# Keys and values of heads 4 to 7 as pairs in seven products, and old-cache logits by wide products and sums, in a float32 hybrid decoder step

## The chip, the cores and the metric

The kernel runs on one core of one Trainium2 chip. The core has a matrix engine (TensorE, PE), a vector engine (VectorE, DVE), a scalar engine (ScalarE, ACT), GpSimd (POOL), and SyncE (SP), which here only issues DMA. The metric is the device time of one execution in microseconds (us); the time of a kernel is the median of several executions. One execution is also recorded by the hardware profiler. Times in the profile count from the start of the recorded span.

## The reference

One inference step of a decoder layer with two parallel branches, on 512 prompt tokens with 16 learned meta tokens ahead of them, and on 8 sample sequences of 4 new tokens each, which have 512 old positions in a paged cache. Everything is float32; the model width is 2048, with 8 heads of 128.

```python
h = rmsnorm(x, g_pre)
q, k, v, ga, cb, cc, ch, gc, ma, mc = jnp.split(h @ w_in, split_offsets(), axis=-1)
a = attend(q, k, v, b_sb).reshape(bsz, t, D_ATTN) * jax.nn.silu(ga)
c = cb * causal_conv(u_ext, w_conv, b_conv) * jax.nn.silu(gc)        # u = cc * ch with its history
merged = (jax.nn.sigmoid(ma + b_gate[:D_MODEL]) * (a @ w_pa)
          + jax.nn.sigmoid(mc + b_gate[D_MODEL:]) * (c @ w_pc))
y = x + rmsnorm(merged @ w_out, g_post)
```

The attention breaks a stick: with z = q k / sqrt(128) + b, the weight of position s for query t is sigmoid(z_ts) times the product of (1 - sigmoid(z_tj)) over the positions j between s and t, worked out in log space. For the samples the keys and values are those of the cache's pages and the new ones. Keys and values of all tokens and the last two inputs of the convolution are outputs too.

## The kernel before, in words

**Matrix products.** A float32 product is made from three products of a faster matrix format. `w_split` (line 237) cuts a block of weights into a high part (`whi`, cast on ScalarE, line 240) and a remainder (`wlo`, a subtraction on VectorE, line 241); the normalised tokens stand in memory in the same two parts, `h_hi` and `h_lo`, 16 blocks of 128 rows by 560 token columns. Each block of the inner dimension takes three matmuls: high by high, high by low, low by high. Three buffers hold split weights (`whl`), five hold loaded ones (`wraw`).

`proj` (line 271) projects onto 128 columns: 16 blocks, two halves of 280 tokens, three matmuls each, so 96 (line 256). `pair` (line 1012) projects onto 256 columns. It cuts weights and tokens into 2 x 2 blocks and forms the result in `seven` (line 974) from seven products of half the inner dimension in place of eight: seven times 8 x 3 = 24 matmuls (line 971), with sums of weight blocks (lines 983, 986, 994, 999) and of results (997, 1002) on VectorE. The block sums of the tokens, `t_hi` and `t_lo`, are made once ahead of the pairs (lines 936 to 956), and the difference of two token blocks then takes the place of one block inside `h_hi` and `h_lo`: direct projections have to be done by then.

**Order of the program.** Norm and queries of heads 0 to 3; then `head_now` for heads 0 to 3: keys, values, the queries of a later head, and attention over the prompt. Then `head_later` for heads 4 to 7: only keys and values, by direct projections, with copies put in DRAM (`k_scr`, `vn_scr`) for their attention later on. Then the token block sums; then 36 pairs: 4 of the attention gate, 16 of the convolution (4 groups of 4), 16 of the two output gates. Behind them come the attention of heads 4 to 7 among the products with `w_pc`, the products with `w_pa`, and the last product with `w_out`, also by sevens.

**The samples' attention over the cache** runs beside this as a generator, `decode_steps` (line 759). It goes through 16 units (two halves of four heads, eight sequences). A unit loads its queries, repeated over all partitions (`qb`), and four pages of keys (`kpage`, three buffers), and forms the logits on VectorE, one instruction per page, query and head: multiply 128 keys-by-channel elements by the query and sum them up (line 781; the sum is written by a second record, the read of the accumulator). That is 16 instructions per page. The generator stops after each page. The calls `dec_step` and `dec_group` (lines 891 to 906) place its steps in the program: the first `DEC1` = 6 units among heads 0 to 7, the other ten among the first 25 pairs; behind them come the weights (after pairs 26 to 28) and the products with the values.

**What sets the order.** A planner orders the instructions of each engine by its own costs; the order of the program counts among those that are ready in its plan. `pin` (`keep_in_program_order`) ties an instruction behind the one written before it on the same engine, so that it can't be moved ahead of that one. At run time each engine and each DMA queue works strictly in the planned order. Loads of weights go through SP's queue; page loads and all stores of this stage go through POOL's queue, so a page load that waits for a buffer holds up what stands behind it.

Of the kernel before, what the change touches and what calls it, by code (L numbers as in the profile page):

```python
# [17 lines left out]
P = 128  # L18
# [24 lines left out]
H = 8  # L43
# [4 lines left out]
DEC1 = 6  # L48
# [12 lines left out]
def hybrid_step_kernel(  # L61
# [499 lines left out]
    def k_proj(h):  # L561
        o = proj(GATE_K + h * P, ALL)
        kr = hp.tile([P, T], F32, name="raw", bufs=2)
        for ob, s in nparts(o):
            act.copy(kr[:, s], ob)
# [6 lines left out]
        pe.matmul(zz, lhsT=kr[:, TP:T], rhs=qs_all[:, h, :], start=True, stop=True)  # L572
# [4 lines left out]
    def v_proj(h, pl=None):  # L577
        o = proj(GATE_V + h * P, ALL)
        vr = hp.tile([P, T], F32, name="raw", bufs=2)
        for ob, s in nparts(o):  # L580
            act.copy(vr[:, s], ob)
# [5 lines left out]
        if pl is None:  # L587
            pool.dma_start(vn_scr[h][0:512].rearrange("(a p) d -> p a d", p=P), vn[:, 0:4, :])
            pool.dma_start(vn_scr[h][512:TP], vn[0:16, 4, :])
            return None  # L590
        return v_split(pl, vn)
# [126 lines left out]
    def head_now(h):  # L718
# [40 lines left out]
    def decode_steps():  # L759
# [3 lines left out]
        for said, part in (("part", units[:DEC1]), ("logits", units[DEC1:])):  # L763
            with tc.tile_pool(name="dec1", bufs=2, side="right") as d1:
                for hf, b in part:
# [8 lines left out]
                    for pg in range(NPG):  # L774
                        kt = d1.tile([P, 512], F32, name="kpage", bufs=3)
                        first(page_load(kt, kc, b, pg, cs))
                        for i, qt in enumerate(qts):
                            for t in range(2):
                                for h in range(4):
                                    junk = d1.tile([P, P], F32, name="junk", bufs=2)  # L780
                                    dve.tensor_tensor_reduce(  # L781
                                        out=junk, in0=kt[:, h * P:(h + 1) * P], in1=qt[:, t, h * P:(h + 1) * P],
                                        scale=1.0, scalar=0.0, op0=ALU.mult, op1=ALU.add,
                                        accum_out=z_all[:, pg, b, 4 * hf + h, 2 * i + t:2 * i + t + 1])
# [713 lines left out]
```

## Time and profile before

| | |
|---|---|
| time before, median of 3 runs (lowest, highest) | 1581.93 us (1581.13, 1584.88) |
| the profiled execution, its own time | 1584.74 us |
| span of its trace | 1583.1 us |
| TensorE busy | 1560.7 us |
| VectorE busy | 1268.5 us |
| ScalarE busy | 761.7 us |
| first and last logit instruction of line 781 | 122.0 us, 945.5 us |

How to read the rows below. In the groups a row names line, engine, operation, output <- inputs, shapes and count; behind the bar stand the busy time in us and the mean of one in ns, then the idle time of the engine just before them and what ended it. In sums by stage there is a stretch of time and for each engine its busy time with the number of instructions; then the granted clock of TensorE as a share (`PEclk`), the busy share of the DMA engines, and the rate. The rows in order of time have the start, the duration, engine, line and operation. A waits row says which engine and line waited for which, for how long in total, how often, and the longest. Matmul ends are modelled, so a matmul's busy time says less than the step from one start to the next.

### The profile page before, as it was taken

The page shows a single profiled execution, that of the slowest core. Times are in us where ns is not written, and L with a number is a line of the kernel's source. Part 1 is how long each engine was busy: PE and PEld are TensorE (multiplying, and loading weights), DVE is VectorE, ACT ScalarE, POOL GpSimd, SP SyncE. Part 2 cuts the span into 40 slices and gives each one's busy share as a digit, 9 for nine tenths or more (in the row PEclk, how much of TensorE's full clock was granted, in tenths as well). Part 3 has the DMA queues.
Part 4 walks back from the last instruction along what each step waited for, and adds up shares of the span by engine and source line. Part 5 has one row for each costly group of instructions (what it writes and reads, how often), then busy time and mean ns, then how long its engine had stood idle before and what let it go on. Part 6 is the DMA issues. An engine that isn't in the chain of part 4 may idle for free.

```text
span 1583.1 us, 32334 instructions
## 1 busy us (share of the span) xinstructions
PE 1560.7 (99%) x12172; PEld 1527.5 (96%) x12172; DVE 1268.5 (80%) x3574; ACT 761.7 (48%) x1345; POOL 234.7 (15%) x428
## 2 busy tenths in 40 slices
PE   8999999999999999999999999999999999999997
PEld 7999999999999999999999999898899999999997
DVE  7329999956799999999999997565678857877776
ACT  6245555435444444444444457444476734345552
POOL 1123333222111010011011102312100010000000
PEclk9999999999999999999999999999999999999999
DMA  8245556344454544445465545767595455433345
GB/s 263 82 137 186 168 160 184 107 130 136 150 180 124 151 130 140 146 134 162 120 181 173 162 138 168 245 194 226 157 306 172 148 178 165 152 107 94 101 143 183
DMA packets 300674, 252.77 MB, mean 160 GB/s; under 512 B 11521, under 2 KB 268613, under 8 KB 299701
## 3 DMA queue, kind: packets, MB, share of 16 engines
q1 hardware_dynamic: 272021, 160.45, 35.1%
q0 software_dynamic: 28368, 89.98, 17.0%
q8 instruction: 95, 1.56, 0.4%
q14 instruction: 62, 0.51, 0.1%
q10 hardware_dynamic: 128, 0.27, 0.1%
HBM read 217.95 MB, written 32.71 MB: 158 GB/s over the span
## 4 chain that ended last, share of the span: by engine, by line
PE 94%; DVE 2%; ACT 1%; DMA 1%; issue 1%; DVEq 0%; SPq 0%; ACTq 0%
PE mm L971 32%; PE mm L256 27%; PE o L971 24%; PE mm L321 2%; PE z L702 1%; PE o L714 1%; PE z L321 1%; PE tp L856 1%; DMA raw<-in_w_in 1%; PE z L620 1%; PE z L1439 1%; PE tp L505 0%; PE z L1293 0%; DVE wlo L241 0%; DMA at<-a_scr 0%
## 5 line engine op out<-in xcount | busy, mean ns | idle before, releaser
L240 ACT CAST whi<-raw 128x1024 fp32r<-128x1024 f32 x247 | 259.4, 1051 | 375.5 <-PE mm L971 135.0
L241 DVE TENSOR_TENSOR wlo<-raw,whi 128x1024 fp32r<-128x1024 f32 x247 | 301.7, 1222 | 90.2 <-ACT whi L240 88.0
L971 PE MATMUL mm<-h_hi,whi 128*128 128x272 f32 (+1 forms) x1152 | 333.5, 289 | 0.7 <-ACT whi L240 0.7
L971 PE MATMUL mm<-h_hi,wlo 128*128 128x272 f32 (+1 forms) x1152 | 332.6, 290 | 0.0
L971 PE MATMUL mm<-h_lo,whi 128*128 128x272 f32 (+1 forms) x1152 | 332.5, 289 | 0.0
L971 PE MATMUL o<-t_hi,whi 128*128 128x272 f32 (+1 forms) x864 | 251.6, 291 | 3.3 <-DVE c L997 3.3
L971 PE MATMUL o<-t_lo,whi 128*128 128x272 f32 (+1 forms) x864 | 251.2, 291 | 0.0
L971 PE MATMUL o<-t_hi,wlo 128*128 128x272 f32 (+1 forms) x864 | 251.1, 291 | 0.0
L781 DVE CUSTOM_DVE_ANT_0 junk<-kpage,qb 128x128 f32<-128x128 f32 x1024 | 246.0, 287 | 4.0 <-DMA qb<-q_scr 3.7
L971 PEld LDWEIGHTS mm<-h_hi,whi 128*128 128x128 f32 x1152 | 217.4, 189 | 6.1 <-ACT whi L240 3.5
L971 PEld LDWEIGHTS mm<-h_lo,whi 128*128 128x128 f32 x1152 | 216.8, 188 | 0.9 <-issue 0.8
L971 PEld LDWEIGHTS mm<-h_hi,wlo 128*128 128x128 f32 x1152 | 217.0, 189 | 0.2
L240 ACT CAST whi<-s 128x1024 fp32r<-128x1024 f32 x126 | 132.0, 1048 | 151.2 <-PE mm L971 48.5
L241 DVE TENSOR_TENSOR wlo<-s,whi 128x1024 fp32r<-128x1024 f32 x126 | 154.2, 1224 | 62.8 <-ACT whi L240 61.3
L256 PE MATMUL mm<-h_lo,whi 128*128 128x280 f32 (+1 forms) x640 | 187.6, 293 | 0.0
L256 PE MATMUL mm<-h_hi,wlo 128*128 128x280 f32 (+1 forms) x640 | 187.1, 293 | 0.0
L256 PE MATMUL mm<-h_hi,whi 128*128 128x280 f32 (+1 forms) x640 | 186.7, 292 | 0.0
L971 PEld LDWEIGHTS o<-t_hi,whi 128*128 128x128 f32 x864 | 164.1, 190 | 4.0 <-DVE c L997 4.0
L971 PEld LDWEIGHTS o<-t_hi,wlo 128*128 128x128 f32 x864 | 164.5, 190 | 0.9 <-issue 0.8
L971 PEld LDWEIGHTS o<-t_lo,whi 128*128 128x128 f32 x864 | 164.8, 191 | 0.0
L256 PEld LDWEIGHTS mm<-h_lo,whi 128*128 128x128 f32 x640 | 120.3, 188 | 0.8
L256 PEld LDWEIGHTS mm<-h_hi,wlo 128*128 128x128 f32 x640 | 120.5, 188 | 0.5
(452 smaller groups left out, 3166.7 us busy)
## 6 DMA issues: line engine op xcount, KB each, us to landing
raw<-in_w_in SPq DMA_DIRECT2D x192, 512.0 KB, 4.5
kpage<-in_cache_k POOLq DMA_DIRECT2D x64, 256.0 KB, 3.8
qb<-q_scr POOLq DMA_DIRECT2D x32, 512.0 KB, 5.7
vpage<-in_cache_v POOLq DMA_DIRECT2D x64, 256.0 KB, 5.7
raw<-in_w_out SPq DMA_DIRECT2D x32, 512.0 KB, 4.0
gate_scr<-g POOLq DMA_DIRECT2D x32, 272.0 KB, 4.9
gt<-gate_scr POOLq DMA_DIRECT2D x16, 544.0 KB, 4.5
raw<-in_w_pc SPq DMA_DIRECT2D x16, 512.0 KB, 4.7
```

The source lines that it names most:

```text
L240: act.copy(hi, x)
L241: dve.tensor_sub(lo, x, hi.bitcast(F32))
L256: pe.matmul(o, lhsT=w, rhs=r[:, t0:t1], start=(k == 0 and n == 0), stop=(k == nk - 1 and n == 2))
L321: pin(pe.matmul(o, lhsT=l, rhs=r[:, k, t0:t1], start=(start and m == 0), stop=(stop and m == 2), skip_group_check=True))
L620: pe.matmul(zt[:m, c0:c0 + n], lhsT=l[:, s0:s0 + m], rhs=r[:, ts:ts + n], start=(c0 == 0 and i == 0), stop=(i == 2), skip_group_check=True)
L702: pe.matmul(o, lhsT=l, rhs=x, start=False, stop=(i == len(ops) - 1), skip_group_check=True)
L714: pe.matmul(ot[:, ts - NMETA:ts - NMETA + n], lhsT=l[:m, st, :], rhs=x[:m, c0:c0 + n], start=False, stop=(g == GROUPS[-1] and i == 2), ski ...
L781: dve.tensor_tensor_reduce(out=junk, in0=kt[:, h * P:(h + 1) * P], in1=qt[:, t, h * P:(h + 1) * P], scale=1.0, scalar=0.0, op0=ALU.mult, o ...
L856: pin(pe.matmul(po[32 * j:32 * (j + 1), :], lhsT=lhs, rhs=rhs, start=(pg == 0), stop=last and n >= len(vts) - 4, tile_position=(0, 32 * j) ...
L971: pe.matmul(o, lhsT=l[:, k, :], rhs=r, start=(start and k == 0 and m == 0), stop=(stop and k == 7 and m == 2), skip_group_check=True)
L1439: pin(pe.matmul(o, lhsT=(m1, m2)[h][:, k + 8 * (q == 1), ts], rhs=two[h][q == 2][:, :, k, :], start=(n == 0), stop=(n == 47)))
```

## The change

Three things change together.

1. `head_later` is replaced by `heads_later`: keys of heads 4 and 5, values of heads 4 and 5, then the same for heads 6 and 7, each as a `pair` in seven products. These four pairs stand behind the token block sums, which are 280 columns wide per half now (274 before), and ahead of the gates. The projections of the queries of heads 4 to 7 leave `head_now` and stand directly behind it.
2. A page's logits: for each half of its four queries one product of 128 x 1024 elements with the page repeated (`kq`), then a sum along the channels on VectorE; of the second half's two queries the second is summed on ScalarE by four accumulating copies. Products and sums on VectorE are pinned.
3. The generator stops four times a page. `DEC1` is 2: two units among heads 0 to 3, fourteen among the pairs, one step after each of the seven products and at the end of a pair (`dec_tick`), from the second pair to the 29th of now 40. The weights come after pairs 30 to 32.

Also, the mask for the later heads (`after`) is made later, and the token sums are formed in another order.

```diff
-DEC1 = 6
+DEC1 = 2
...
@@ head_now
         khi, klo = k_split(np_, k_proj(h))
-        dec_step(1 if h else 0, "part")
+        qhi, qlo = q_split(np_, qr)
+        dec_step(4 if h else 1, "part")
         vhi, vlo = v_proj(h, np_)
-        dec_step(1, "part")
-        q_proj(NOW + h)
-        dec_step(2, "part")
-        ot = next(attend(np_, h, khi, klo, vhi, vlo, *q_split(np_, qr)))
-        dec_step(2, "part")
+        dec_step(4, "part")
+        ot = next(attend(np_, h, khi, klo, vhi, vlo, qhi, qlo))
...
-    def head_later(h):
-        pool.dma_start(k_scr[h], k_proj(h))
-        dec_step(2, "part")
-        v_proj(h)
-        dec_step(2, "part")
+    def heads_later(h, qs):
+
+        for c, out in ((GATE_K, "k"), (GATE_V, "v")):
+            raws = [hp2.tile([P, T], F32, name="raw", bufs=2) for _ in range(2)]
+            seen = []
+            for m, half, b in pair(c + h * P, HC):
+                act.copy(raws[m][:, NMETA + half * HQ:NMETA + (half + 1) * HQ], b[:, HM:])
+                act.copy(raws[m][:, half * HM:(half + 1) * HM], b[:, :HM])
+                seen.append(m)
+                if seen.count(m) < 2:
+                    continue
+                if out == "k":
+                    pool.dma_start(k_scr[h + m], raws[m])
+                    k_out(hp2, h + m, raws[m], qs[:, h + m - NOW, :])
+                else:
+                    vn = v_out(hp2, h + m, raws[m])
+                    pool.dma_start(vn_scr[h + m][0:512].rearrange("(a p) d -> p a d", p=P), vn[:, 0:4, :])
+                    pool.dma_start(vn_scr[h + m][512:TP], vn[0:16, 4, :])
+            dec_group()
...
@@ decode_steps, per page
+                        if pg == 0 and (hf, b) == part[0]:
+                            yield
                         for i, qt in enumerate(qts):
-                            for t in range(2):
-                                for h in range(4):
-                                    junk = d1.tile([P, P], F32, name="junk", bufs=2)
-                                    dve.tensor_tensor_reduce(
-                                        out=junk, in0=kt[:, h * P:(h + 1) * P], in1=qt[:, t, h * P:(h + 1) * P],
-                                        scale=1.0, scalar=0.0, op0=ALU.mult, op1=ALU.add,
-                                        accum_out=z_all[:, pg, b, 4 * hf + h, 2 * i + t:2 * i + t + 1])
-                        yield
+                            kq = d1.tile([P, 2, 4, P], F32, name="kq", bufs=2)
+                            pin(dve.tensor_mul(kq, qt.rearrange("p t (h d) -> p t h d", d=P),
+                                               kt.rearrange("p (h d) -> p h d", d=P).unsqueeze(1)
+                                               .broadcast_to([P, 2, 4, P])))
+                            yield
+                            nt = 2 - i
+                            zt = z_all[:, pg, b, 4 * hf:4 * hf + 4, 2 * i:2 * i + nt]
+                            if i:
+                                for h in range(4):
+                                    act.activation(kq[:, 1, h], kq[:, 1, h], AF.Copy,
+                                                   accum_out=z_all[:, pg, b, 4 * hf + h, 3:4])
+                            pin(dve.reduce_sum(zt.rearrange("p h t -> p t h"), kq[:, 0:nt], axis=mybir.AxisListType.X))
+                            yield
...
@@ dec_group
-        if n <= 25:
-            dec_step((0, 2, 2, 2)[n - 1] if n <= 4 else 1 if n <= 20 else 4, "logits")
-        else:
-            dec_step(2 if n in (26, 28) else 1)
+        if n == 1:
+            dec_step(1, "logits")
+        elif n == 29:
+            dec_step(64, "logits")
+        elif n > 29:
+            dec_step(2 if n in (30, 32) else 1)
+
+    def dec_tick():
+
+        if 1 <= n_group[0] < 29:
+            dec_step(1, "logits")
...
     for h in range(NOW, H):
-        head_later(h)
+        q_proj(h)
     dec_step(64, "part")
...
@@ seven
         product(x, w_split(w11), rb(0, 0), True, False)
+        tick()
         dve.tensor_add(s, w21, w22)
         product(q, w_split(s), rb(0, 1), True, False)
+        tick()
...
@@ ahead of the gates
+    with tc.tile_pool(name="heads2", bufs=1) as hp2:
+        qs = hp2.tile([P, H - NOW, TS], F32, name="qs")
+        for h in range(NOW, H):
+            pool.dma_start(qs[:, h - NOW, :], qt_scr[h][:, PQ:TQ])
+        for h in range(NOW, H, 2):
+            heads_later(h, qs)
```

More of the change, by code (lines that the diff above doesn't have):

```diff
@@ L559, in v_split, with raw_of, k_out @@
         return vhi, vlo
[L561 to L563 removed]
+    def raw_of(o):
+        raw = hp.tile([P, T], F32, name="raw", bufs=2)
         for ob, s in nparts(o):
[L565 removed]
+            act.copy(raw[:, s], ob)
+        return raw
+    def k_out(hp, h, kr, qs):
         kn = hp.tile([P, 5, P], F32, name="nat", bufs=2)
@@ L571, in k_proj, with v_out @@
         zz = z_ps()[0:TS, 0:TS]
-        pe.matmul(zz, lhsT=kr[:, TP:T], rhs=qs_all[:, h, :], start=True, stop=True)
+        pe.matmul(zz, lhsT=kr[:, TP:T], rhs=qs, start=True, stop=True)
         act.activation(z_new[:, :, h, :], zz.rearrange("p (b t) -> p b t", t=DT), AF.Identity,
                        bias=bsb[0:TS, h:h + 1])
-        return kr
[L577 to L581, printed above, removed]
+    def k_proj(h):
+        kr = raw_of(proj(GATE_K + h * P, ALL))
+        k_out(hp, h, kr, qs_all[:, h, :])
+        return kr
+    def v_out(hp, h, vr):
         vn = hp.tile([P, 5, P], F32, name="nat", bufs=2)
@@ L948, in hybrid_step_kernel @@
             t_split(part(t_hi[0]), part(t_lo[0]), x)
+        for c in range(0, 8, 2):
+            x, y = part(x1), tsp.tile([P, 2, HC], F32, name="y")
             dve.tensor_sub(y, part(h_f, 0, 0), x)
```

41 lines of the change are left out of this document (23 added, 18 removed).

## The prediction

> **What bounds the kernel now.** I read the page first (shares of the engines and the chain that ended last), then sums by stage, then the order in time on VectorE (DVE) and TensorE (PE) inside the stage that the change fills.
>
> ```profile
> PE 1560.7 (99%) x12172; PEld 1527.5 (96%) x12172; DVE 1268.5 (80%) x3574; ACT 761.7 (48%) x1345; POOL 234.7 (15%) x428
> DVE  7329999956799999999999997565678857877776
> PE 94%; DVE 2%; ACT 1%; DMA 1%; issue 1%; DVEq 0%; SPq 0%; ACTq 0%
> ```
>
> TensorE sets the end: 94% of the chain. The 80% of VectorE is an average; slices 4 to 8 and 12 to 23 stand at 9. The stages, cut where the work changes (us from the start; busy time of each engine):
>
> ```profile
> core 0: us, PE busy (x) PEld busy (x) DVE busy (x) ACT busy (x) POOL busy (x), PEclk, DMA share, GB/s
> 75.00:365.00 290.00, 290.00 (x2231) 283.09 (x2230) 227.89 (x1014) 138.23 (x280) 88.47 (x164) 1.00 0.50 151
> 440.00:946.00 506.00, 505.18 (x4000) 504.76 (x4000) 485.65 (x1634) 227.82 (x336) 52.44 (x91) 1.00 0.50 148
> 946.00:1170.00 224.00, 222.24 (x1734) 204.50 (x1734) 143.51 (x171) 116.43 (x166) 48.63 (x87) 0.99 0.68 209
> ```
>
> From 440 to 946 us lie pairs in seven products (gates and convolution) with most of the old-cache logits between them. There VectorE works 485.65 of 506 us: TensorE is still the bound, with 20 us to spare. After 946, when the logits are done, VectorE has 80 us idle in 224. The pace of TensorE, from the chain in order of time (start, length, what):
>
> ```profile
> 211.11 8.99 PE mm L256 x70
> ...
> 454.73 5.83 PE mm L971 x46
> ...
> 944.86 5.79 PE mm L971 x46
> ```
>
> A matmul of 280 columns costs 8.99/70 = 0.1284 us. Between the two lower rows lie 23 pairs: (944.86 - 454.73)/23 = 21.31 us for a pair of 7 x 24 = 168 matmuls. The stage holds 4000/168 = 23.8 pairs.
>
> How VectorE spends its time there (start, duration, what; instructions overlap, so the step from start to start is the price, not the duration):
>
> ```profile
> 444.97 1.23 DVE L983 TENSOR_TENSOR s<-raw 128x1024 f32<-128x1024 f32 x1
> 446.11 0.29 DVE L781 CUSTOM_DVE_ANT_0 junk<-kpage,qb 128x128 f32<-128x128 f32 x1
> 446.32 0.09 DVE L781 DVE_READ_ACCUMULATOR2_ANT z_all<- 128x1 f32 x1
> 446.32 0.29 DVE L781 CUSTOM_DVE_ANT_0 junk<-kpage,qb 128x128 f32<-128x128 f32 x1
> 446.53 0.08 DVE L781 DVE_READ_ACCUMULATOR2_ANT z_all<- 128x1 f32 x1
> 446.53 1.22 DVE L241 TENSOR_TENSOR wlo<-raw,whi 128x1024 fp32r<-128x1024 f32 x1
> 447.67 1.22 DVE L994 TENSOR_TENSOR raw<-raw 128x1024 f32<-128x1024 f32 x1
> 448.80 0.29 DVE L781 CUSTOM_DVE_ANT_0 junk<-kpage,qb 128x128 f32<-128x128 f32 x1
> ```
>
> A two-tensor operation on 1024 elements steps on after 1.14, 1.14 and 1.13 us, 0.09 us before its shown end. A logit instruction steps on after 0.21 us, the read of its accumulator included, although 0.29 and 0.09 are shown for the two. One page for four heads is 16 of them: 3.36 us, not the 6 us to which the durations add up.
>
> **The change, part by part.**
>
> *Matmuls removed.* Keys and values of heads 4 to 7 are eight projections of 2 x 16 x 3 = 96 matmuls of 280 columns; as four pairs they are 4 x 168 = 672 in place of 768. 96 x 0.1284 = 12.3 us less on the bounding engine. Their transposes, outputs and products with the sample queries stay.
>
> *VectorE inside the K and V pairs.* A pair has seven remainders of casts, four block sums of 1024 and two subtractions, where two direct projections had four remainders.
>
> ```profile
> L997 DVE TENSOR_TENSOR c<-o,s 128x272 f32<-128x272 f32 x28 | 12.3, 439 | 4.4 <-PE o L971 4.4
> L511 DVE COPY ks<-tp 32x128 f32<-32x128 f32 x16 | 4.3, 270 | 0.0
> ```
>
> A subtraction steps on after 0.44 - 0.09 = 0.35 us, a small copy of the natural layout after 0.2. That is 11 x 1.14 + 0.7 = 13.2 us against 4.6; with two logit pages (below, 8.1) and four small copies, 22.1 us. TensorE needs 168 x 0.1284 = 21.6 us and the transposes on top:
>
> ```profile
> 356.12 0.60 PE L505 MATMUL tp<-ident,raw 128*128 128x128 f32 x4
> 356.65 0.25 PE L572 MATMUL z<-qs_all,raw 128*32 128x32 f32 x2
> 356.83 0.40 PE L256 MATMUL mm<-h_lo,whi 128*128 128x280 f32 x1
> ```
>
> 356.12 to 356.83 is 0.71 us, with the two small transposes about 1 us per head: 23.6 us for a pair. VectorE fits under it with 1.5 us, so I charge nothing; without that cover, 4 pairs x 2 us.
>
> *A logit page.* Removed: 16 instructions, 3.36 us. Added: two products of 1024 elements, a sum over 1024, a sum over 512, and four accumulating copies on ScalarE. A product with a repeated operand stands nowhere in the trace; its nearest row is the plain product, 1.14, which I take. Nor is there a sum of this width; the nearest:
>
> ```profile
> L1315 DVE TENSOR_REDUCE ss<-og_a x3: 167/171/203, 1563.1 to 1573.0; 128x1 f32<-128x16 f32 x2, 128x3 f32<-128x48 f32 x1
> L1286 ACT ACTIVATE sq<-z x62: 257/278/384, 1407.8 to 1572.5; 128x128 f32<-128x128 f32 x60, 128x256 f32<-128x256 f32 x2
> L1286 ACT ACTIVATION_READ_ACCUMULATOR sq<-z x62: 184/194/201, 1408.0 to 1572.8; 128x1 f32 x62
> ```
>
> ```profile
> L473 DVE TENSOR_SCALAR lo<-e 128x416 f32<-128x416 f32 x12 | 4.5, 372 | 0.8 <-ACT r L470 0.8
> L474 DVE TENSOR_TENSOR lo<-e,lo 128x416 f32<-128x416 f32 x12 | 7.1, 591 | 0.1
> ```
>
> The small reductions take about 169 ns for 16 elements and 203 for 48: 1.06 ns for each further element. So 1024 elements take 169 + 1008 x 1.06 = 1.24 us and step on after 1.15, 512 after 0.61. A page is then 2 x 1.14 + 1.15 + 0.61 = 4.04 us. Bounds: at the rate of a one-input operation (591 - 372 = 219 ns saved on 416 elements, 0.53 ns each, 0.8 us on 1536) it is 3.2 us; above, if a sum costs a tenth more than its slope says, 4.2 us. I take 4.04, since the row is of the operation itself. So the wide form costs VectorE 0.7 us more per page, even with a quarter of the sums on ScalarE.
>
> The Trainium skill (VectorE: DVE Perf Modes, "Rules for kernel authors") speaks for such a rewrite: chained operations should not be fused for speed, their number should be kept small, since each pays its own drain. The steps of 0.21 us above are shorter than the shown durations, so the trace doesn't bear it out for these. What it would give is a rival below.
>
> *Where the pages lie.* Before, 24 pages belong to heads 0 to 3 and 40 to the pairs; now 8 and 56. The ticks run in 28 pairs, the last three of K and V and 25 behind them, eight to a pair; four make a page: two pages a pair. Taking 16 pages out of heads 0 to 3 frees VectorE there, but TensorE is busy 290.00 of 290.00 us, so nothing is won. The queries of heads 4 to 7 move from inside these heads to behind them. They cover the token block sums, 13 x 4 operations of 0.65 us:
>
> ```profile
> L934 DVE TENSOR_TENSOR t_lo<-x,t_hi 128x548 fp32r<-128x548 f32 x8 | 5.7, 719 | 1.4 <-ACT t_hi L933 1.4
> ```
>
> 34 us under four projections of 96 x 0.1284 = 12.3 us; I charge nothing. Heads 0 to 3 lose a quarter of what fills their waits on exponentials: nothing, or up to 3 us a head.
>
> *The 25 gate and convolution pairs with ticks.* Work other than logits on VectorE in the stage: 485.65 - 605 x 0.21 = 358.6 us, over 23.8 pairs 15.07 us each (the logits' 605 instructions with as many accumulator reads are the 1210 of this row, overlaps included):
>
> ```profile
> 440.00:946.00 506.00, 148.28 (x1210) 1.00 0.50 148
> ```
>
> With two pages: 15.07 + 8.08 = 23.15 us a pair against 21.31 on TensorE. 25 x 1.84 = 46 us too much. The products and sums are tied behind the last VectorE instruction written before them and are ready (three page buffers), so I expect them to run in their place; the next remainder then comes later, and TensorE waits for it.
>
> ```profile
> POOL kpage L757 <- DVE z_all L781: 277.9, 33, 16.1
> ACT whi L240 <- PE mm L971: 84.1, 70, 1.8
> DVE wlo L241 <- ACT whi L240: 13.2, 37, 1.0
> ```
>
> To this come VectorE's own waits for a cast, 13.2 us in this stage (last row): 14 us for 25 pairs, between none and twice that. ScalarE's waits for a free weight slot (second row) vanish. Three slots let two products of 3 us run ahead once: -6.
>
> *Queues.* Page loads already make POOL's queue wait up to 16.1 us (first row). A page now lives four ticks, 10.7 us; the outputs of a K or V pair stand behind these loads, and the single buffer of the sample rows makes VectorE's copy of the second head wait for them. Hidden as long as the planner spaces them; if not, up to 3 us for each of 4 pairs. ScalarE gets four copies and four accumulator reads a page, at most 4 x 0.47 = 1.9 us, 3.8 of a pair's 21.3, beside 227.82 of 506 us: room enough, though a cast may stand behind them. The other edits (wider token blocks, a separate query tile, the later mask) come to under 1 us in idle time.
>
> *Sum:* -12.3 + 46 + 14 - 6 = +42 us. The profiled execution took 1584.74 us (span 1583.1), so 1626.7; it lies 2.8 us above the median of the runs shown, 1581.93, on which I put the prediction: 1624 us.
>
> **The rivals.**
>
> *ScalarE's accumulations delay the casts as well.* Two quartets a pair, each up to 1.9 us ahead of a cast; were half of that lost in 25 pairs: 25 x 2 x 0.9 = 45 us in place of the 14 counted, so 1624 + 31 = 1655 us. For it: the cast of a block sum can't be issued early, and its engine works in order. Against: other remainders can fill the gap.
>
> *The logits fall back rather than hold up the weights.* The tie keeps an instruction from being early, not from being late. If the planner lets them slip, the 60 us too much go into the 80 us that VectorE has idle after 946, and only the removed matmuls show: 1581.9 - 12.3 = 1570 us. It decides as long as the products with the values behind the logits still end before the gates do. Against: the loads are ahead, so the steps are ready in their place.
>
> *Small instructions pay in full.* If each logit instruction cost its shown 0.29 + 0.09 us, a page would fall from 6.1 to 2 x 1.22 + 1.24 + 0.70 = 4.4 us, the stage's other work would be 485.65 - 605 x 0.38 = 256 us, 10.7 a pair, and 10.7 + 8.8 = 19.5 us would fit under 21.31: 1570 us. Sums at the one-input rate come out the same within 4 us (15.07 + 6.4 = 21.5). Against: the steps, and the slope of the reductions. This is the case of the Trainium skill's rule named above.
>
> *About even.* Two thirds of the overload hidden by deeper running ahead, the waits filled: 15 - 12.3 = +3, 1585 us.
>
> **How the numbers follow.** Overload as summed 0.58 (its own range 1593 to 1646: 3.7 to 4.2 us a page, waits of 0 to 28 us); casts late as well 0.15; logits fall back 0.13; cheap pages 0.07; about even 0.07. Under 0.3% (4.7 us) a measurement of this kernel can't tell from no change. Faster 0.20, within 0.05, slower 0.75 (0.58, 0.15 and the upper part of the even case). The range goes from the cheap end, 1570, to the second case, 1655.
>
> **What would show it.** Right: in the convolution pairs TensorE's waits end at the remainder of L241 on VectorE; a pair takes 23 us or more there; VectorE has next to no idle time while the logits last; the wide products step on after 1.14 us, the sums after 1.15 and 0.61; the 280-wide direct matmuls are 768 fewer, those of pairs 672 more. Wrong: pairs keep 21.3 us; the logits end well after the 29th pair; a sum of 1024 steps on in under 0.8 us; or TensorE waits in heads 0 to 3, which have fewer projections to fill them.

## Result and profile after

The changed kernel takes 1673.57 us, the median of four runs (1669.96 to 1676.09), against 1581.53 us before: a ratio of 1.0576, with a 95% interval of 1.0551 to 1.0602. It is slower, by 92 us, where 42 us had been forecast (1624 us). The profiled execution took 1669.96 us with a span of 1668.4; the span before was 1583.1, so the two traces differ by 85.3 us, and this is the difference that the readings below divide up.

The page of the changed kernel, its busy times, the slices of VectorE and of the granted clock, and the chain that ended last:

```profile
PE 1573.3 (94%) x12076; PEld 1526.1 (91%) x12076; DVE 1334.2 (80%) x1818; ACT 849.8 (51%) x1879; POOL 237.9 (14%) x432
...
DVE  7257667799899999999999997665668876887776
...
PEclk9999997899999999999999999999999999999999
...
PE 49%; DVE 18%; issue 7%; ACT 4%; DMA 4%; POOL 1%; DVEq 0%; SPq 0%; POOLq 0%; ACTq 0%
```

There are 96 matmuls fewer, as counted (12172 to 12076). TensorE is busy 94% of the span and no longer 99%, and its share of the chain falls from 94% to 49%. VectorE stands at 9 in all but one of the slices 9 to 24, and in slices 7 and 8 the granted clock dips to 7 and 8 tenths. The stages show two places (us from the start; busy time of PE, PEld, DVE, ACT, POOL with counts; granted clock):

```profile
core 0: us, PE busy (x) PEld busy (x) DVE busy (x) ACT busy (x) POOL busy (x), PEclk, DMA share, GB/s
75.00:265.00 190.00, 189.37 (x1440) 183.23 (x1439) 116.59 (x192) 106.65 (x263) 54.06 (x105) 1.00 0.40 120
265.00:303.00 38.00, 0.00 (x0) 0.00 (x0) 37.28 (x56) 12.69 (x25) 2.53 (x5) 0.56 0.01 2
...
485.00:830.00 345.00, 322.02 (x2419) 313.21 (x2418) 333.31 (x393) 164.66 (x429) 36.77 (x63) 0.98 0.46 138
830.00:1005.00 175.00, 166.07 (x1265) 162.31 (x1264) 165.86 (x186) 93.31 (x222) 18.31 (x32) 0.98 0.50 149
1005.00:1246.00 241.00, 240.66 (x1898) 223.25 (x1898) 154.47 (x173) 122.11 (x171) 49.89 (x89) 1.00 0.63 194
```

**The hole.** From 265 to 303 us TensorE runs not one matmul, while VectorE is busy 37.28 of 38 us. What stands there, VectorE in order of time (start, duration, what; a count joins equal neighbours):

```profile
265.39 0.69 DVE L804 TENSOR_REDUCE z_all<-kq 128x4 f32<-128x512 f32 x1
266.70 2.69 DVE L972 TENSOR_TENSOR r<-h_hi 128x560 f32<-128x560 f32 x4 [0.62 <-ACT kq L802]
269.31 2.69 DVE L973 TENSOR_TENSOR r<-r,h_lo 128x560 f32<-128x560 f32 x4
...
279.75 0.73 DVE L961 TENSOR_TENSOR h_lo<-r,h_hi 128x560 fp32r<-128x560 f32 x1
...
299.31 1.38 DVE L961 TENSOR_TENSOR t_lo<-x,t_hi 128x560 fp32r<-128x560 f32 x2
300.72 1.23 DVE L1015 TENSOR_TENSOR s<-raw 128x1024 f32<-128x1024 f32 x1
```

and TensorE:

```profile
264.10 0.27 PE L538 MATMUL tp<-ident,qr 128*32 128x128 f32 x1
303.14 0.60 PE L1002 MATMUL mm<-h_hi,whi 128*128 128x280 f32 x1 [38.76 <-ACT whi L240]
```

These are the sums of the token blocks, 52 operations in 34 us. They begin when the last logit page ahead of them ends (266.1 us) and end at 300.7; only then comes the weight sum `s` of the first pair's second product, its cast, and at 303.14 TensorE goes on. That product does not need all of these sums: the token block that it reads is complete at 280.5 us (the row of `h_lo`), and its weights had landed by 247.8. So the last 20 us of the hole are, as far as the rows show, the place of `s` in VectorE's order, behind all 52 sums. The query projections had all run by then: they filled the waits of the attention in heads 0 to 3 and ended at 261 us. Before, the same sums lay like this:

```profile
290.56 2.65 DVE L943 TENSOR_TENSOR r<-h_hi 128x548 f32<-128x548 f32 x4
293.13 1.36 DVE L944 TENSOR_TENSOR r<-r,h_lo 128x548 f32<-128x548 f32 x2
294.41 0.27 DVE L510 COPY nat<-tp 16x128 f32<-16x128 f32 x1
```

There too they began behind the last early page (290.5 us), but under direct projections of keys and values that lasted until 365 us.

**The pairs.** In the convolution stage, 485 to 830 us, 2419 matmuls make 2419/168 = 14.4 pairs of 345/14.4 = 24.0 us; before it was 506/(4000/168) = 21.25 by the same reckoning. VectorE has 11.7 us idle in 345. There run 57 sums of logits, so 28.5 pages, 1.98 a pair. The first of the 25 gate and convolution pairs with ticks, and the pair after the last (TensorE, first matmul of each):

```profile
396.37 0.29 PE L1002 MATMUL mm<-h_hi,whi 128*128 128x272 f32 x1
...
991.49 0.29 PE L1002 MATMUL mm<-h_hi,whi 128*128 128x272 f32 x1
```

(991.49 - 396.37)/25 = 23.80 us a pair, 62 us more in all than 25 at 21.31. TensorE is busy 558.25 of these 595.12 us. So 37 us of the 62 are idle time; the rest lies in matmuls that step on more slowly behind the waits (last section). What ended the waits, from 400 to 1005 us:

```profile
ACT whi L240 <- DVE s L1019: 14.0, 13, 3.8
...
PE o L1002 <- ACT whi L240: 13.0, 10, 1.6
...
PE mm L1002 <- ACT whi L240: 9.4, 21, 0.8
```

TensorE waits for casts of weights on ScalarE (22.4 us), and casts in turn wait for a weight sum on VectorE (14.0 us).

So the 85.3 us between the traces are -12.3 (matmuls) + 38 (hole) + 62 (pairs) - 2.4 for everything else.

The costs of the new operations, VectorE's groups by line (busy, mean ns of one | idle ahead of them), and a stretch of a convolution pair:

```profile
L794 DVE TENSOR_TENSOR kq<-qb,kpage 128x1024 f32<-128x1024 f32 x128 | 155.2, 1214 | 0.2 <-DMA qb<-q_scr 0.2
L804 DVE TENSOR_REDUCE z_all<-kq 128x8 f32<-128x1024 f32 x64 | 77.2, 1207 | 0.0
L804 DVE TENSOR_REDUCE z_all<-kq 128x4 f32<-128x512 f32 x64 | 43.2, 676 | 0.0
```

```profile
563.16 1.22 DVE L241 TENSOR_TENSOR wlo<-s,whi 128x1024 fp32r<-128x1024 f32 x1
564.30 1.22 DVE L804 TENSOR_REDUCE z_all<-kq 128x8 f32<-128x1024 f32 x1
565.43 0.44 DVE L1133 TENSOR_TENSOR cv<-o,cv 128x272 f32<-128x272 f32 x1
565.77 0.68 DVE L804 TENSOR_REDUCE z_all<-kq 128x4 f32<-128x512 f32 x1
566.37 0.44 DVE L1039 TENSOR_TENSOR c<-mm,s 128x272 f32<-128x272 f32 x1
566.72 1.22 DVE L1019 TENSOR_TENSOR s<-s,raw 128x1024 f32<-128x1024 f32 x1
567.85 0.44 DVE L1133 TENSOR_TENSOR cv<-c,cv 128x272 f32<-128x272 f32 x1
569.05 1.23 DVE L241 TENSOR_TENSOR wlo<-s,whi 128x1024 fp32r<-128x1024 f32 x1 [0.76 <-ACT whi L240]
570.19 1.22 DVE L794 TENSOR_TENSOR kq<-qb,kpage 128x1024 f32<-128x1024 f32 x1
571.32 1.22 DVE L241 TENSOR_TENSOR wlo<-raw,whi 128x1024 fp32r<-128x1024 f32 x1
```

The sum of 1024 steps on after 565.43 - 564.30 = 1.13 us and the sum of 512 after 566.37 - 565.77 = 0.60; the product after 571.32 - 570.19 = 1.13, at the median of all 1.14. A page is 2 x 1.14 + 1.13 + 0.60 = 4.01 us. The row at 569.05 shows the price of a full VectorE: the remainder comes after a gap of 0.76 us, because its cast had waited for the sum `s` (566.72) behind the work of the page. TensorE waited 1.60 us for the same cast.

### The profile page after: what moved, and what is told of

Same layout as the page of the kernel before. It is cut to its first block, busy times and chain, and to the rows that moved or that the text cites. A ratio compares the mean times of both kernels' runs of the same rounds, so it can differ in the third digit from the quotient of the medians.

```text
span 1668.4 us, 30901 instructions
## 1 busy us (share of the span) xinstructions
PE 1573.3 (94%) x12076; PEld 1526.1 (91%) x12076; DVE 1334.2 (80%) x1818; ACT 849.8 (51%) x1879; POOL 237.9 (14%) x432
## 3 DMA queue, kind: packets, MB, share of 16 engines
q0 software_dynamic: 28496, 90.05, 16.3%
## 4 chain that ended last, share of the span: by engine, by line
PE 49%; DVE 18%; issue 7%; ACT 4%; DMA 4%; POOL 1%; DVEq 0%; SPq 0%; POOLq 0%; ACTq 0%
PE mm L1002 19%; PE o L1002 15%; PE mm L256 11%; DVE wlo L241 5%; DVE kq L794 3%; DVE z_all L804 3%; DMA raw<-in_w_in 3%; ACT whi L240 2%; DMA qb<-q_scr 1%; PE tp L876 1%; DVE s L1015 1%; DVE s L1019 1%; DVE raw L1029 1%; PE z L1484 1%; PE o L715 1%
## 5 line engine op out<-in xcount | busy, mean ns | idle before, releaser
L1002 PE MATMUL mm<-h_hi,whi 128*128 128x272 f32 (+2 forms) x1280 | 375.3, 293 | 53.5 <-ACT whi L240 48.9
L1002 PE MATMUL mm<-h_lo,whi 128*128 128x272 f32 (+2 forms) x1280 | 371.4, 290 | 0.0
L1002 PE MATMUL mm<-h_hi,wlo 128*128 128x272 f32 (+2 forms) x1280 | 369.1, 292 | 1.6 <-DVE wlo L241 1.5
L1002 PE MATMUL o<-t_hi,whi 128*128 128x272 f32 (+2 forms) x960 | 284.8, 297 | 19.5 <-ACT whi L240 13.0
L1002 PE MATMUL o<-t_hi,wlo 128*128 128x272 f32 (+2 forms) x960 | 283.0, 295 | 0.4 <-DVE wlo L241 0.4
L1002 PE MATMUL o<-t_lo,whi 128*128 128x272 f32 (+2 forms) x960 | 281.1, 293 | 0.0
L1002 PEld LDWEIGHTS mm<-h_hi,wlo 128*128 128x128 f32 x1280 | 241.3, 190 | 2.8 <-DVE wlo L241 2.6
L794 DVE TENSOR_TENSOR kq<-qb,kpage 128x1024 f32<-128x1024 f32 x128 | 155.2, 1214 | 0.2 <-DMA qb<-q_scr 0.2
L804 DVE TENSOR_REDUCE z_all<-kq 128x8 f32<-128x1024 f32 (+1 forms) x128 | 120.5, 941 | 0.1
L256 PE MATMUL mm<-c_hl,whi 128*128 128x272 f32 x512 | 100.1, 289 | 1.2 <-DVE gt L1253 1.2
```

Of the source, the lines that this page charges most:

```text
L256: pe.matmul(o, lhsT=w, rhs=r[:, t0:t1], start=(k == 0 and n == 0), stop=(k == nk - 1 and n == 2))
L794: pin(dve.tensor_mul(kq, qt.rearrange("p t (h d) -> p t h d", d=P), kt.rearrange("p (h d) -> p h d", d=P).unsqueeze(1) .broadcast_to([P, 2 ...
L804: pin(dve.reduce_sum(zt.rearrange("p h t -> p t h"), kq[:, 0:nt], axis=mybir.AxisListType.X))
L1002: pe.matmul(o, lhsT=l[:, k, :], rhs=r, start=(start and k == 0 and m == 0), stop=(stop and k == 7 and m == 2), skip_group_check=True)
```

## The experiments

Two questions were open: whether the pairs are long because VectorE has too much work, and what makes the hole. The ratios of the first four are against the kernel before at 1581.87 us; the others have the runs beside them at 1581.67 and 1581.36 us.

### Early pages stepped ahead of head 3's attention

```diff
         vhi, vlo = v_proj(h, np_)
-        dec_step(4, "part")
+        dec_step(64 if h == NOW - 1 else 4, "part")
         ot = next(attend(np_, h, khi, klo, vhi, vlo, qhi, qlo))
```

> The changed kernel, with the logit steps of the first two units all written ahead of the attention of head 3, so that none is left behind the queries of heads 4 to 7. Theory M (the token block sums start late because their memory is still held by the last page of these logits, which is tied behind the queries of head 7): the sums then run under the four query projections, TensorE's hole of 38 us between 265 and 303 us falls below 5 us, and the time goes from 1673.6 to about 1639 us. Rival S (34 us of block sums on VectorE stand ahead of the first weights of the first K pair whenever that pair comes next): the hole stays, 1670 to 1674 us.

Measured: 1670.6 us, ratio 1.0556 (1.0532 to 1.0581). Moving the pages alone wins nothing, as the second expectation has it. The last early page now ends at 245.9 us and the first sums start at 248.4, but TensorE's standstill is only divided; its waits from 245 to 305 us:

```profile
PE mm L1002 <- ACT whi L240: 22.4, 1, 22.4
PE z L703 <- ACT l L494: 8.0, 1, 8.0
```

The high and low parts of the token blocks (`t_hi`, `t_lo`) are allocated where the pool of heads 0 to 3 was closed, and their attention ends only at 279.8 us. So there is, as it seems, a second condition beside the last page, and what follows it on VectorE still runs until 299.8 us with no projection left.

### The old narrow logits in place of the wide ones, tied in the same way

```diff
-    pin(dve.tensor_mul(kq, qt..., kt...broadcast_to([P, 2, 4, P])))
...
-    pin(dve.reduce_sum(zt.rearrange("p h t -> p t h"), kq[:, 0:nt], axis=mybir.AxisListType.X))
+    for t in range(2):
+        for h in range(4):
+            pin(dve.tensor_tensor_reduce(out=junk, in0=kt[...], in1=qt[...], ..., accum_out=z_all[...]))
+        yield
```

> The changed kernel with the old logit instructions (multiply and sum over 128 elements, 16 per page), four at each tick and tied like the wide ones; nothing on ScalarE. The hole is left in. Theory O (the pairs are slow because the wide page is more work for VectorE than fits): a page falls from 4.0 to 3.36 us, a pair from 23.8 to 15.07 + 6.72 + 0.55 = 22.3 us, 25 pairs give 37 us: about 1636 us. Rival T (the pairs are slow because the steps are tied in place and can't fill waits): pairs stay at 23.8 us, 1668 to 1674 us.

Measured: 1608.99 us, ratio 1.0167 (1.0138 to 1.0196). The hole is as before (the last remainder of the blocks ends at 300.7 us). In the convolution stage:

```profile
485.00:830.00 345.00, 345.00 (x2734) 344.76 (x2734) 333.29 (x1071) 148.16 (x226) 33.77 (x59) 1.00 0.48 140
```

TensorE is busy all the time and a pair takes 345/(2734/168) = 21.2 us, with VectorE as busy as under the wide logits (333.29 and 333.31 us). But fewer pages run beside each pair: the 748 records of logits in this stretch are 23.4 pages in 16.3 pairs, 1.44 a pair and not 1.98. The narrow steps fell back behind the weights: the last one runs at 1050 us, 123 us after the 29th pair ended (926.9). That costs little later: from 1050 to 1200 us, where the values are due, TensorE is busy 146.67 of 150 us. The time is below both expectations, 27 us under the lower: that narrow steps would keep the whole pace of TensorE was in neither. The kernel takes 64.6 us less than with wide steps, and this has two parts that the run does not separate: a page costs less, and fewer of them stand beside a pair. An estimate from the rows: at 1.98 pages a pair narrow steps would ask 15.07 (the other work of a pair, from the prediction) + 1.98 x 3.36 = 21.7 us of VectorE, and wide ones at 1.44 a pair 15.07 + 1.44 x 4.01 = 20.8, less than TensorE's 21.3.

### Wide steps without the ties

```diff
-    pin(dve.tensor_mul(kq, ...))
+    dve.tensor_mul(kq, ...)
-    pin(dve.reduce_sum(zt..., kq[:, 0:nt], ...))
+    dve.reduce_sum(zt..., kq[:, 0:nt], ...)
```

(with the early pages ahead of head 3's attention, as in the first experiment)

> The first experiment's kernel (steps of the first two units ahead of the attention of head 3) with the wide products and sums no longer tied. Theory O: VectorE's work per pair stays at 23.1 us, only its waits can be filled, so 0 to 14 us less than the first experiment, 1625 to 1639 us. Rival T: with steps free to fill waits the pairs go back to 21.3 us: 1639 - 62 = 1577 us.

Measured: 1713.78 us, ratio 1.0829 (1.0805 to 1.0854). Both expectations are missed, by far and upwards:

```profile
485.00:830.00 345.00, 292.80 (x2063) 280.25 (x2063) 343.47 (x398) 163.31 (x495) 41.89 (x72) 0.94 0.45 136
```

VectorE is busy 343.47 of 345 us and a pair takes 345/(2063/168) = 28.1 us. Untied, the wide steps run earlier than their ticks (the last at 828 us, not 989) and ahead of the remainders: 78 products are 39 pages in 12.3 pairs, 3.2 a pair, and 15.07 + 3.2 x 4.01 = 27.9 us. When they are done, pairs take 21.3 us again. So the tie did not cause the loss: it limited it. Why the planner puts wide steps ahead of the weights and narrow ones behind them is not settled by these runs.

### Narrow steps without the ties

The same with the narrow instructions, untied.

> The first experiment's kernel with the old logit instructions, not tied: four pairs for K and V, 56 pages among the pairs. Theory O: 15.07 + 6.72 = 21.8 us of VectorE a pair against 21.3 on TensorE, 25 x 0.5 = 12 us over, against the 12.3 us of matmuls saved: 1580 to 1588 us. Rival T: pairs at 21.3 us, 1570 us.

Measured: 1601.14 us, ratio 1.0121 (1.0101 to 1.0142), 13 us above the higher of the expected figures. Pairs take 21.1 to 21.35 us. The sums start at 179 us, right behind the last early page (178.4), and end at 285.9; TensorE still waits once for 21.0 us, where the expectation had no hole; that alone is more than the 13 us missed. The last page runs at 1027 us, behind the pairs with ticks, and TensorE is busy 144.07 of 150 us from 1025 to 1175.

### The work of a page cut, and raised

First the sums on VectorE read 8 of each 128 products (most of the summing is left out):

```diff
-    pin(dve.reduce_sum(zt..., kq[:, 0:nt], axis=mybir.AxisListType.X))
+    pin(dve.reduce_sum(zt..., kq[:, 0:nt, :, 0:8], axis=mybir.AxisListType.X))
```

> The sums on VectorE read 8 of each 128 products instead of all (the logits are then wrong sums: most of the summing is left out); products, accumulations on ScalarE, ties and order stay. Theory L (VectorE has more work in a pair than TensorE): a page falls from 4.0 to about 2 x 1.14 + 2 x 0.2 = 2.7 us, a pair's work to 15.1 + 5.4 = 20.5 us, under TensorE's 21.3; pairs take 21.3 to 21.8 us and the time is 1673.6 - 25 x 2.2 = 1618, 1608 to 1628 us. Theory C (the accumulations on ScalarE stand ahead of the casts of the weights and hold the products up): they are all still there, pairs stay at 23 us or more, 1655 to 1674 us.

then ScalarE's quarter goes to VectorE:

```diff
-    nt = 2 - i
+    nt = 2
...
-    if i:
-        for h in range(4):
-            act.activation(kq[:, 1, h], kq[:, 1, h], AF.Copy, accum_out=z_all[:, pg, b, 4 * hf + h, 3:4])
```

> The quarter of the sums that ScalarE takes goes to VectorE: both sums of a page are over 1024 elements, no accumulating copy on ScalarE. Theory L: a page takes 4.0 + 0.54 us, a pair 1.07 us more; over 25 pairs with ticks and some of the key and value pairs +27 to +30: 1698 to 1706 us. Theory C: without the accumulations the casts are in time, pairs get shorter: 1640 to 1674 us.

Measured, one run each: 1621.92 and 1699.68 us, both in the range of VectorE's work. The convolution stage of the first, then of the second:

```profile
485.00:830.00 345.00, 341.63 (x2676) 338.36 (x2675) 324.16 (x444) 183.21 (x478) 41.34 (x71) 1.00 0.52 152
```

```profile
485.00:830.00 345.00, 313.19 (x2317) 303.02 (x2317) 334.39 (x377) 124.77 (x192) 35.58 (x61) 0.97 0.45 134
```

The 25 pairs take 21.75 us each with the short sums (399.2 to 942.9 us) and 24.86 with all sums on VectorE (399.6 to 1021.1), against 23.80: 1.07 us more had been expected for the second, and 1.06 it is. The first has all accumulations on ScalarE (183.21 us busy) and short pairs, the second has none (124.77) and long ones. The length of a pair follows the work on VectorE; that ScalarE's accumulations hold up the casts is out.

### Heads 4 and 5 direct again, wide logits

```diff
-DEC1 = 2
+DEC1 = 3                       # four early pages more
...
+    for h in (4, 5):
+        head_later(h)          # direct keys and values, four tick steps behind each
     dec_step(64, "part")
...
-    for h in range(NOW, H, 2):
+    for h in range(6, H, 2):
         heads_later(h, qs)
```

> Keys and values of heads 4 and 5 go back to direct projections, behind the queries and ahead of the token block sums; only heads 6 and 7 are two pairs. The wide logits stay, with four pages more ahead of the sums (two pairs fewer carry ticks). Theory H (the 38 us in which TensorE stands still are the token block sums on VectorE, with no projection left that covers them): 192 direct products, 49 us with their neighbours, now cover 34 us of sums, the hole is under 5 us, and the time is 1673.6 - 38 + 6 (48 products more) = 1642, 1636 to 1646 us. Rival R (the hole is a wait for memory, weights or a queue that the first pair meets wherever it stands): the hole stays at 30 us or more, 1668 to 1680 us.

Measured, one run: 1686.93 us, above both ranges. The expectation of the hole fell, and with it the simple reading that cover alone was missing. TensorE's waits around the first pair and VectorE's order:

```profile
PE mm L1012 <- ACT whi L240: 46.0, 1, 46.0
```

```profile
329.70 0.69 DVE L812 TENSOR_REDUCE z_all<-kq 128x4 f32<-128x512 f32 x1
331.01 2.70 DVE L982 TENSOR_TENSOR r<-h_hi 128x560 f32<-128x560 f32 x4 [0.62 <-ACT kq L810]
```

The four early pages written behind the direct projections were drawn along with them, because a tied step follows the last VectorE instruction written before it, and the last of them ended at 330.4 us. The sums started behind it, when the direct projections were over (316.8 us), though VectorE had been idle for much of the time from 261 us on. What starts the sums is the end of the last early page: the pool of their buffers is opened where the pages' pool was closed, and the first of them waits for ScalarE's read of the page's products (`kq`), which it does not use itself.

### Heads 6 and 7 alone as pairs, narrow logits

The kernel before, with this changed and what it needs (token blocks 280 wide and formed in the new order, the later mask, page steps spread over 27 pairs):

```diff
-    for h in range(NOW, H):
+    for h in (4, 5):
         head_later(h)
...
+    for h in range(6, H, 2):
+        heads_later(h, qs)
```

> The kernel before with one thing changed: keys and values of heads 6 and 7 as two pairs in seven products ahead of the gates; heads 4 and 5 stay direct, the logits stay narrow and untied, 40 pages behind the heads as before. If overload and the uncovered sums are the two causes of the loss, neither is here: 48 products fewer, 6.2 us, leave 1575.7, 1573 to 1580 us. If pairs for keys and values cost more by themselves (their transposes, outputs, block sums on VectorE), or the hole comes with any such pair: 1585 us or more.

Measured: 1587.24 us, ratio 1.0033 (1.0021 to 1.0045), against 1575.7 expected without a cost of these pairs, and in the range of the second case (1585 or more). It is the hole again, smaller: the sums start at 290.58 us, 0.1 us behind the last page, as in the kernel before; but with four direct projections fewer the first pair starts at 312.8 and not at 365.5, and finds them unfinished until 328.0:

```profile
PE mm L1001 <- ACT whi L240: 12.9, 1, 12.9
```

### The end of the early pages moved, and the sums left out

Four runs on this reading: 20 and 16 early pages in place of 24 in the kernel just shown; the wide one with heads 4 and 5 direct, all its early pages stepped ahead of head 3's attention; and the changed kernel without the additions and subtractions of the blocks.

```diff
-DEC1 = 6
+DEC1 = 5        # 20 early pages; 4 in the next run; the others go to later pairs
```

> The kernel with heads 6 and 7 as pairs and narrow logits (1587.2 us), with 20 logit pages ahead of the token block sums in place of 24. Theory G (the sums start only when the last of these pages is done, at 290.6 us there, and the first pair finds them unfinished for 14 us): VectorE is through with the pages 4 x 3.36 = 13 us earlier, the sums of the first kind move ahead of the end of head 3's attention (291 us), what must follow it takes about 21 us and ends near 318 us in place of 328; the hole shrinks to 0 to 5 us, and the time is 1573 to 1579 us. Rival K (pairs for keys and values cost 10 us wherever they stand): 1584 to 1590 us.

> The same with 16 pages ahead of the sums and 48 behind them. Theory G: the sums are done before the first pair wants them, no hole, 1572 to 1577 us, as long as the pairs take the 48 pages: 25 x 6.2 + 2 x 8.4 = 172 us of VectorE's spare time are 51 pages of 3.36 us. Where they don't fit, the last pages come late and up to 8 us come back behind the convolution: 1578 to 1584. Rival K: 1584 to 1590 us.

```diff
-        dec_step(4, "part")
+        dec_step(64 if h == NOW - 1 else 4, "part")
         ot = next(attend(...))
```

> The kernel with wide logits and heads 4 and 5 direct (1686.9 us, TensorE still for 47 us), with the 12 early pages all stepped ahead of the attention of head 3, so that none stands behind the covering projections. Theory G: the sums start by 260 us and end under the four direct projections; the hole falls to 5 us or less, 1686.9 - 43 = 1644, 1638 to 1650 us; the pairs keep their 23 to 24 us. Rival R (memory, weights or a queue of the first pair): 1675 us or more.

```diff
-    dve.tensor_sub(r, part(h_f, 0, 0), part(h_f, 0, 1))
-    dve.tensor_add(r, r, part(l_f, 0, 0))
...
-    t_split(part(t_hi[0]), part(t_lo[0]), x)
+    act.copy(r, part(h_f, 0, 1))
+    t_split(part(t_hi[0]), part(t_lo[0]), part(h_f, 1, 1))
...
```

> The changed kernel with the ten VectorE additions and subtractions per quarter that form the token blocks left out (the blocks are then plain copies of the activations, so that the results of all pairs are wrong); casts and remainders of the blocks stay, 16 remainders of 0.65 us in place of 56 instructions. Theory G: the hole shrinks from 38 us to the 10 to 15 us of casts and remainders: 1673.6 - 25 = 1648, 1644 to 1654 us. Rival R: hole and time stay, 1665 to 1674 us.

Measured: 1599.88 us with 20 pages (ratio 1.0117, 1.0100 to 1.0133); **1578.25 us with 16 pages, ratio 0.9974 (0.9960 to 0.9988)**; 1643.16 us for the wide one and 1652.37 us without the block sums, one run each. TensorE's wait at the first pair, with 16 pages, for the wide one, and without the sums:

```profile
PE mm L1001 <- DVE wlo L241: 1.8, 1, 1.8
...
PE mm L1001 <- ACT whi L240: 0.6, 1, 0.6
```

```profile
PE mm L1012 <- ACT whi L240: 4.3, 1, 4.3
```

```profile
PE mm L993 <- ACT whi L240: 13.6, 1, 13.6
```

The end of the last early page, the start of the sums, the end of head 3's attention, the end of the last remainder of the blocks, and the last direct or query projection, all in us:

| kernel | last early page | sums start | attention ends | blocks done | last projection |
|---|---|---|---|---|---|
| before | 290.5 | 290.6 | 291.8 | 365.4 | 365.7 |
| changed | 266.1 | 266.7 | 260.6 | 300.7 | 261.2 |
| early pages first | 245.9 | 248.4 | 279.8 | 299.8 | 258.4 |
| wide, 4 and 5 direct | 330.4 | 331.0 | 264.1 | 365.0 | 316.8 |
| the same, pages first | 274.6 | 274.7 | 289.4 | 321.0 | 314.6 |
| narrow, 24 early pages | 290.5 | 290.6 | 291.8 | 328.0 | 313.0 |
| narrow, 20 | 263.4 | 265.0 | 309.4 | 330.9 | 316.6 |
| narrow, 16 | 239.0 | 239.7 | 290.3 | 315.7 | 314.4 |

The sums start with the last early page in each row, within 3 us. Without the block sums, the remainders, which don't use these buffers, start at 269.0 us, ahead of the end of the last page (271.0). In the table TensorE stands still for about as long as the last column lies ahead of the one before it, to within 3 us (with the early pages first, a part of these 41 us falls between the matmuls of the attention). Three of the four runs came out by it: the wide kernel went from 1686.9 to 1643.2 us (1638 to 1650 expected) when its pages moved, though its sums start at 274.7 us and not by 260; the changed kernel lost 21 us when the sums were left out (1644 to 1654 expected), and with 16 pages the blocks are done 1.3 us after the last projection. That run, at 1578.25, is 1.25 us above the range expected if the pairs take all 48 pages, and in the one expected if the last pages come late (1578 to 1584); the last page ends at 974 us. It is 0.26% faster than the kernel before: pairs for two heads, not four, with old logits, fewer of them ahead of the sums. It leaves pairs for keys and values little cost of their own: 48 matmuls less would give 1581.36 - 6.2 = 1575.2 us, 3 us less than measured, and 2.4 us of that are the waits shown above.

The run with 20 pages missed both theories. Its sums did start earlier, but head 3's attention ended 17.5 us later than with 24 pages, and with it the second half of the blocks' work:

```profile
316.00:335.00 19.00, 5.71 (x39) 4.85 (x38) 18.90 (x29) 7.63 (x14) 7.28 (x13) 0.68 0.15 38
```

Another 14 us went between 953 and 1039 us, where two pairs took 32.4 and 30.1 us in place of some 24. TensorE was busy ahead of 316 us (73.92 of 76 us from 240 on), so it was the order that changed: direct projections went ahead of the attention. Why the planner chose this with 20 pages and not with 16, and what held the two late pairs, stays open.

## Why the prediction was right and wrong

**The step that failed** is the one on the queries that move behind heads 0 to 3: "34 us under four projections of 96 x 0.1284 = 12.3 us; I charge nothing." The 34 us were right. The cover was not there, for two reasons that could be read in the trace of before, the first as a coincidence of two times: the sums start at the end of the last early logit page and not when their inputs are ready (290.5 and 290.6 us), and the 75 us behind that moment are filled with the direct projections that the change takes away. The query projections went ahead as filler for the attention and were gone by 261 us. The missing term is +38 us, and with it the sum would have been +80. The prediction named the test (TensorE waiting around heads 0 to 3, "which have fewer projections to fill them") but gave it no price, and did not write down what the cover costs when it is gone.

**The pairs** were the right mechanism with terms a little too small: 46 + 14 - 6 = 54 us forecast, 62 found. The price of a page was right (4.04 against 4.01 us), and so was the bound: VectorE works in place, with 11.7 us idle in 345, and the last logit sum ends at 990 us, just ahead of the end of the 29th pair (991.5). Of the 23.80 us of a pair, 345 - 11.7 = 333.3 of 345 are work, 23.0 us, where 23.15 were forecast; the idle part is 0.8 us a pair, 20 us in all and not 14, and nothing is seen of the 6 us won back by running ahead. The short and the long pages (21.75 and 24.86 us a pair) show that it is VectorE's work. The bound is two pages a pair as much as the price of a page: 1.44 narrow pages a pair left TensorE its pace, and 3.2 wide ones made pairs of 28.1 us. Two smaller readings were wrong. TensorE's waits were to end at the remainder; they end at the cast (22.4 us, against 1.1 at the remainder), since the weight sum ahead of the cast is late too. And ScalarE's waits for a free weight slot did not vanish: of the row of 84.1 us quoted, 25.0 are left from 400 to 1005 us.

**Right as charged:** the 96 matmuls, and the key and value pairs, of which the three behind the first take 23.6 to 24.6 us (23.6 forecast).

**The rivals.** "Casts late as well" gave 1655 us, nearest to the time, but by a mechanism that is not there: without ScalarE's accumulations pairs get longer, by the 1.06 us that VectorE's added work accounts for. Casts are late, but behind VectorE's weight sums. "The logits fall back" is what the narrow steps do (21.2 us a pair with the ties left in place), and not the wide ones; the doubt was right and was about the wrong form. "Small instructions pay in full" is out, as 16 of them are cheaper by 0.65 us a page than the four wide steps: the Trainium skill's advice in VectorE: DVE Perf Modes, "Rules for kernel authors", not to fuse for speed and to keep the number of operations small, is not borne out here, with 0.21 us for a step that multiplies and sums 128 elements. For each element and pass the wide steps are the cheaper ones (1.14 us for 1024 is 1.1 ns, 0.21 us for 128 is 1.6 ns); what they lose is the second pass, 3584 elements a page gone through and not 2048. "About even" needed the overload hidden; it was not.

The last 6 us of the miss lie between the profiled executions and the medians: the one of before is 2.8 us above the median on which the forecast was put, the one of after (1669.96 us) 3.6 below its own (1673.57).

## What to carry to other kernels

When a change takes work off the bounding engine, look up what ran beside that work on the other engines, and when that other work can start: its start may hang on a buffer (here the logit pages' and, as it seems, the attention's), not on its inputs. Price the uncovered stretch even if you think that it is covered. And compare the steps from start to start of the old and the new form on the engine that will be nearly full: here four wide steps cost 4.0 us where sixteen narrow ones cost 3.36. Multiply by how many are tied into a stretch: two pages a pair asked more of VectorE than a pair of TensorE lasts, and what was over went on to TensorE, the waits included.

## What the runs showed of the hardware

A sum over 1024 elements into 8 takes VectorE as long as a two-input product of 1024 (1207 and 1214 ns shown, 1.13 and 1.14 us from start to start).

In the 38 us without a matmul the granted clock is 0.56, and TensorE starts slowly behind them:

```profile
305.03 0.43 PE L1002 MATMUL mm<-h_lo,whi 128*128 128x280 f32 x1
305.26 0.43 PE L1002 MATMUL mm<-h_hi,wlo 128*128 128x280 f32 x1
305.50 0.43 PE L1002 MATMUL mm<-h_hi,whi 128*128 128x280 f32 x1
```

A matmul of 280 columns steps on after 0.23 us there and not 0.128; the first product behind the hole takes 308.4 - 303.1 = 5.3 us where 24 x 0.128 = 3.1 would do. So a hole costs about 2 us more than its length (0.4 of it a wait for the first remainder).

A much shorter wait had the same effect. Behind the waits of 1.60 and 0.43 us at 567.5 and 569.6 us the granted clock is 0.50 from 569.7 to 573.0 us, and matmuls of 272 columns step on after 0.23 us and not 0.125; from 573.2 on it is 1.00 again.
